# A streaming-encoder trunk: values read into their own tiles, an embedding in two halves, a shared norm tile, a free list of raw buffers, pair evictions at high priority

## The chip, the cores and the metric

The kernel runs on one core of one Trainium2 chip. The core has a matrix engine (TensorE, in the profile PE, with its weight loads as PEld), a vector engine (VectorE, DVE), a scalar or activation engine (ScalarE, ACT), GpSimd (POOL) and SyncE (SP), which here only issues transfers. Each engine runs its own instructions in the order in which they stand in its queue, and waits on semaphores for the others. Sixteen DMA engines move data between HBM and the on-chip memory. The metric is the device time of one execution in microseconds; the time before is the median of three.

## What is computed

Two layers (DEPTH 2) work on 512 frames of width 1024, in float32. Cut to what matters:

```python
for i in range(DEPTH):
    h = rmsnorm(x, norm1_g[i])
    z = h @ w_in[i] + b_in[i]        # mLSTM q k v o i f, retention q k v g, two branch gates
    y_m = sigmoid(mo) * headnorm(mlstm(mq, mk, mv, mi, mf))        # 4 heads of 256
    y_r = silu(rg) * headnorm(retention(rope(rq), rope(rk), rv))   # 4 heads, values of 512
    merged = sigmoid(gm) * (y_m @ w_bm[i]) + sigmoid(gr) * (y_r @ w_br[i])
    x = x + merged @ w_out[i]
    h2 = rmsnorm(x, norm2_g[i])
    x = x + square(relu(h2 @ w_ff1[i] + b_ff1[i])) @ w_ff2[i] + b_ff2[i]
    h3 = rmsnorm(x, norm3_g[i])
    x = x + sigmoid(h3 @ w_pe_gate[i]) * (p[i] @ w_pe[i])          # the embedding: p[i] has 256 columns
return rmsnorm(x, final_g)
```

## The kernel before

**Products.** Every float32 operand is split into a high and a low half of type fp32r, and a product is three matmuls: high by high, high by low, low by high (`mm3`, L440). The high half is written by ACT as a copy, the low half by DVE as a subtraction (`split`, L284: ACT L286, DVE L287).

**Units.** All weights stream from HBM once, in the order of `unit_list` (L160 and on). A T8 unit is 128 output columns by 1024 rows (`t8`, L451). A PAIR unit makes 256 output columns with seven products of half the size in place of eight (the Winograd form of Strassen's scheme, `run_pair`, L474). Its weights come in three raw tiles A, C and B; a fourth, D, is formed on chip. Its products P1, P5, P6, P2, P3, P7 and P4 are of 12 matmuls of 256 columns each and share three PSUM banks: a is used by P1, P6, P7 and P4 in turn, c by P5 and P3, b by P2. A product that starts anew in a bank that another has filled waits until that one is evicted. P4 is deferred: it is put on the list `later`, and `flush` runs it after P1 and P5 of the next pair, or inside the next T8. The retention values of two heads are a WIDE unit (`run_wide`, L513), the embedding has two PE units.

**Weights on their way.** `fill_raws` (L361) loads raw tiles through SP's queue; there are four buffers (RAWS, tag wr) and, until w_out, one more (wrx). `prep_next` (L389) runs LOOK = 2 units ahead: it splits a raw tile into the halves that PE reads, and for a pair adds parts of A and C into B (L421) and forms D (L424). The sums of weight blocks that the pairs need are made in HBM by accumulating transfers, which POOL issues at a pace set by PE (L331).

**Evictions.** For a projection pair `pair_tiles` (L541) empties the banks into two tmp tiles: P1, P5, P6 and P4 by ACT (L548, L550, L554, L560), P2, P3 and P7 by DVE (L552, L556, L558). For a pair of the second feed-forward matrix `add` in `ff2` (L1394) adds each bank into x on DVE (L1400). The ring of tmp tiles has six (NTMP). These instructions stand on ACT's and DVE's queues among the splits of the next weights. The order on each engine is that of a list scheduler, which follows the order of the program unless a priority is given.

**Retention.** The values of heads 1 and 3 are made with those of heads 0 and 2 and wait in HBM (rv_spill, written at L1166). `rv_load` (L1192) reads them back: for each of four row tiles it takes a tmp tile, issues a load on POOL's queue (L1197), and splits the tile into the value tiles that the head before has used. In the order of a layer (L1283 and on), head 0 is attended, its gates made, then `rv_load(1)`; head 2 is attended, r_qk(3) and the eight tiles br of the first half of w_br are made, each copied by ACT (L1301) and stored to br_spill by a transfer on ACT's queue (L1302), and then comes `rv_load(3)`, scores, and the gates and outputs of head 2 (`r_out`), whose pairs the trace calls l0r2o0 and l0r2o1. In the same way l0r0o0 is the first gate pair of head 0; l0r1brq and l0r1brk are head 1's query and key pairs.

**Norms.** A norm's sum of squares (tag ssum, written at L630 to L642) and its spread factor (tag rb, L702) are two tiles of 512 columns in a pool that lives throughout.

**End of a layer.** The feed-forward pairs of the last block come after the two embedding units (L1443): eight tiles of six matmuls with 512 columns, copied to `pe` by ACT. The four pairs l0o30 to l0o33 follow, then `flush` runs the last pair's P4, and after it the last two tiles of the third norm's operand are made (`tile3`, L1388). The gate projection w_pe_gate uses them at once; its evictions use the six or seven tmp tiles of a new pool.

## Time and profile before

| | |
|---|---|
| median of 3 runs | 2348.01 us (2347.84 to 2348.44) |
| the profiled execution | 2347.49 us |
| its span in the profile | 2345.8 us |
| granted TensorE clock, mean over the span | 0.997 |
| PE busy | 99% of the span, 13,660 matmuls |
| DVE, ACT, POOL busy | 73%, 52%, 10% |
| moved by DMA | 394.89 MB, 168 GB/s in the mean |

Times in the profile are counted from the span's start. A busy engine is one that has an instruction running; matmuls overlap, so two that follow each other start sooner than the first one's shown duration. In the table of waits a row says which instruction of PE stood idle, for which other engine's instruction, for how long in total, how often, and the longest. In a timeline row come start, duration, engine, line, operation, the tile written and the tiles read; in brackets, the idle time before it and what ended that. A row of windows gives the busy time of each engine in a stretch, the clock that TensorE was granted (1.00 is full), the busy share of the DMA engines and the rate in GB/s.

### The profile page before, as it was taken

How to read it: one execution, taken by the hardware profiler on the slowest of the kernel's cores; microseconds unless marked ns; L12 is line 12 of the kernel's file. 1: busy time of each engine (PE TensorE's matmuls, PEld its weight loads, DVE VectorE, ACT ScalarE, POOL GpSimd, SP SyncE). 2: the span in 40 equal slices, each digit the busy share in tenths (PEclk: the TensorE clock that was granted, in tenths of full speed). 3: DMA queues.
4: the chain of work that ended last, by engine and by line, in shares of the span. 5: the costliest groups of instructions: out<-in, count | busy, mean ns of one | idle time of the engine just before them, and what ended most of it. 6: DMA issues, size and time to landing. Idle time of an engine off the chain costs nothing. (4 is left out here: it accounts for less than half of the span.)

```text
span 2345.8 us, 35261 instructions
## 1 busy us (share of the span) xinstructions
PE 2320.2 (99%) x13660; PEld 2056.2 (88%) x13660; DVE 1722.9 (73%) x2658; ACT 1218.9 (52%) x1768; POOL 245.7 (10%) x369
## 2 busy tenths in 40 slices
PE   9999999999999999999999999999999999999998
PEld 7888899898898898899888888998989988998997
DVE  7878767895675577677878787778958656776785
ACT  6656444553554445446557564454536445445454
POOL 3111101100102100000321110000000020000012
PEclk9999999999999999999999999999999999999999
DMA  5666676667578667676775645434343542433431
GB/s 201 187 180 172 218 229 170 205 189 202 168 230 269 195 198 189 199 219 181 206 221 169 182 124 186 136 126 158 108 158 104 166 153 96 130 108 98 132 117 59
DMA packets 146631, 394.89 MB, mean 168 GB/s; under 512 B 15376, under 2 KB 18832, under 8 KB 146464
## 3 DMA queue, kind: packets, MB, share of 16 engines
q1 hardware_dynamic: 99952, 247.77, 32.0%
q0 software_dynamic: 31104, 117.45, 20.4%
q10 hardware_dynamic: 15408, 27.43, 3.3%
q8 instruction: 107, 1.75, 0.3%
q14 instruction: 60, 0.49, 0.1%
HBM read 373.71 MB, written 123.73 MB: 212 GB/s over the span
## 5 line engine op out<-in xcount | busy, mean ns | idle before, releaser
L286 ACT ACTIVATE wh<-wr 128x1024 fp32r<-128x1024 f32 (+1 forms) x223 | 232.2, 1044 | 276.5 <-issue 69.6
L287 DVE TENSOR_TENSOR wl<-wr,wh 128x1024 fp32r<-128x1024 f32 (+1 forms) x221 | 271.9, 1232 | 77.7 <-ACT wh L286 77.5
L286 ACT ACTIVATE wh_B<-wr 128x1024 fp32r<-128x1024 f32 x100 | 105.9, 1059 | 159.2 <-PE l0f L443 8.5
L287 DVE TENSOR_TENSOR wl_B<-wr,wh_B 128x1024 fp32r<-128x1024 f32 x100 | 121.9, 1219 | 32.5 <-ACT wh_B L286 32.3
L286 ACT ACTIVATE wh_D<-wr 128x512 fp32r<-128x512 f32 x76 | 48.0, 632 | 124.9 <-DVE wr L424 65.4
L286 ACT ACTIVATE wh_C<-wr 128x1024 fp32r<-128x1024 f32 x76 | 80.2, 1056 | 61.3 <-issue 9.2
L286 ACT ACTIVATE wh_A<-wr 128x1024 fp32r<-128x1024 f32 x76 | 79.9, 1052 | 54.7 <-PE l1f L443 9.0
L287 DVE TENSOR_TENSOR wl_C<-wr,wh_C 128x1024 fp32r<-128x1024 f32 x76 | 94.3, 1240 | 18.7 <-ACT wh_C L286 18.5
L287 DVE TENSOR_TENSOR wl_A<-wr,wh_A 128x1024 fp32r<-128x1024 f32 x76 | 92.7, 1220 | 17.3 <-ACT wh_A L286 17.3
L442 PE MATMUL l1f<-l1n2h,wh 128*128 128x512 f32 x256 | 99.8, 390 | 0.0
L442 PE MATMUL l0f<-l0n2h,wh 128*128 128x512 f32 x256 | 99.8, 390 | 0.0
L444 PE MATMUL l0f<-l0n2h,wl 128*128 128x512 f32 x256 | 99.7, 389 | 0.0
L444 PE MATMUL l1f<-l1n2h,wl 128*128 128x512 f32 x256 | 99.7, 389 | 0.0
L443 PE MATMUL l1f<-l1n2l,wh 128*128 128x512 f32 x256 | 99.6, 389 | 0.0
L443 PE MATMUL l0f<-l0n2l,wh 128*128 128x512 f32 x256 | 99.6, 389 | 0.0
L287 DVE TENSOR_TENSOR wl_D<-wr,wh_D 128x512 fp32r<-128x512 f32 x76 | 52.4, 689 | 33.2 <-ACT wh_D L286 31.7
L421 DVE TENSOR_TENSOR wr<-wr,wr 128x512 f32<-128x512 f32 x76 | 52.1, 686 | 14.6 <-DMA wr<-wpairs 13.1
L444 PEld LDWEIGHTS l0f<-l0n2h,wl 128*128 128x128 f32 x256 | 48.0, 188 | 10.2
L444 PEld LDWEIGHTS l1f<-l1n2h,wl 128*128 128x128 f32 x256 | 48.1, 188 | 10.1
L443 PEld LDWEIGHTS l1f<-l1n2l,wh 128*128 128x128 f32 x256 | 48.1, 188 | 9.8
L442 PEld LDWEIGHTS l0f<-l0n2h,wh 128*128 128x128 f32 x256 | 48.1, 188 | 9.8
L442 PEld LDWEIGHTS l1f<-l1n2h,wh 128*128 128x128 f32 x256 | 48.1, 188 | 9.7
(5625 smaller groups left out, 8357.9 us busy)
## 6 DMA issues: line engine op xcount, KB each, us to landing
wr<-wstream SPq DMA_DIRECT2D x219, 512.0 KB, 4.2
wr<-wpairs SPq DMA_DIRECT2D x228, 256.0 KB, 2.8
wr<-wwide SPq DMA_DIRECT2D x24, 512.0 KB, 4.0
s0t<-wwide POOLq DMA_DIRECT2D x5, 1024.0 KB, 7.8
s4t<-wwide POOLq DMA_DIRECT2D x5, 1024.0 KB, 9.0
s12t<-wwide POOLq DMA_DIRECT2D x5, 1024.0 KB, 8.1
s16t<-wwide POOLq DMA_DIRECT2D x5, 1024.0 KB, 8.5
s1t<-wpairs POOLq DMA_DIRECT2D x4, 1024.0 KB, 6.7
```

Of the source, the lines that this page charges most:

```text
L286: a = ac.activation(hi_ap, src, AF.Copy)
L287: return a, ve.tensor_sub(lo_ap, src, hi_ap.bitcast(F32))
L421: ve.tensor_tensor(raws[n, "B"][:, Q:], kept.pop((n, "A"))[:, Q:], r[:, :Q], OP.add)
L442: te.matmul(o, sh, mh, start=first, stop=False)
L443: te.matmul(o, sh, ml, start=False, stop=False)
L444: cur["mm"] = te.matmul(o, sl, mh, start=False, stop=last)
```

## The change

It has five parts. (1) `rv_load` becomes `rv_fetch`, which issues the four loads straight into the low tiles of the values, right behind the attend that has used them, and `rv_split`, which splits them in place after the next head's scores; no tmp tile is used. (2) The embedding is in two halves: `embed(0)` before the last four feed-forward pairs, `embed(1)` behind them, and the last pair's P4 runs after the second tile of `embed(1)`. The order of the weight units follows. (3) A norm's sum and spread share one tile of 1024 columns (`nr`), handed from norm to norm (`own`). While no norm needs it, from the unit rv0 to w_out, it is a raw buffer for weights ("one"). (4) Raw buffers are an explicit list: four of the weight pool, "low" and "one"; `give` returns a buffer when its last reader has been issued, and the next load takes the first that fits. (5) Pair evictions and the adds of `ff2` are issued at a priority of 250 ahead of their place in the program.

```diff
...
 LOOK = 2
+AHEAD = 250
 WARM = 11
...
     u.append(("PE", 0))
+    pairs(ff_order()[1])
     u.append(("PE", 1))
-    pairs(ff_order()[1])
     full("w_pe_gate")
...
     room = unit_list(0).index(("T8", "w_out", 0, 0))
-    cur["room"], cur["more"] = (), None
+    wide0 = unit_list(0).index(("WIDE", (0, "rv0"), 0))
+    where = {n + i * NU // L: ("low", "one") if n >= wide0 else ("low",) for i in range(L) for n in range(room)}
+    free, taken = ["low", "one"] + list(range(RAWS)), {}
+
+    def norm_tile():
+        return opool.tile([P, 2 * T], F32, name="nr", tag="nr", bufs=1)
+
+    def raw_tile(a):
+        if a == "one":
+            return norm_tile()
+        pl, tag = (cur["low"], "wrx") if a == "low" else (wpool, f"wr{a}")
+        return pl.tile([P, UN], F32, name=f"wr{at['load']}", tag=tag, bufs=1)
...
-    def fill_raws(most=RAWS + 1):
-        while at["load"] < len(loads) and len(raws) + len(kept) < most:
+    def fill_raws(most=None):
+        while at["load"] < len(loads) and at["load"] != most:
             n, x = loads[at["load"]]
-            r = None
-            if n in cur["room"] and cur["more"] not in raws:
-                cur["more"] = n, x
-                r = cur["low"].tile([P, UN], F32, name=f"wr{at['load']}", tag="wrx", bufs=1)
-            elif len(raws) - (cur["more"] in raws) >= RAWS:
+            fits = where.get(n, ()) if n * L // NU == cur["layer"] else ()
+            a = next((a for a in free if a in range(RAWS) or a in fits), None)
+            if a is None:
                 break
-            raws[n, x] = r = r or wpool.tile([P, UN], F32, name=f"wr{at['load']}", tag="wr", bufs=RAWS)
+            free.remove(a)
+            taken[n, x] = a
+            raws[n, x] = r = raw_tile(a)
             if x:
...
         fill_raws()
+
+        def give(*a):
+            free.extend(taken.pop(k) for k in a)
...
             kept[n, x] = r
+        elif x == "D":
+            give((n, "B"))
         elif x == "C":
...
             ve.tensor_tensor(raws[n, "B"][:, Q:], kept.pop((n, "A"))[:, Q:], r[:, :Q], OP.add)
+            give((n, "A"), (n, "C"))
         elif x == "B":
...
             formed[n, ("t4", x[1])] = t
+            give((n, ("t2", x[1])), (n, x))
+        elif not wide or x[0] != "t4":
+            give((n, x))
...
+    def ahead():
+
+        return tc.high_priority(AHEAD)
+
     def pair_tiles(name, act, consume, y=None):
...
         def done(x, o):
+            with ahead():
+                evict(x, o)
+            if x == "P4":
+                consume(y)
+
+        def evict(x, o):
             if x == "P1":
...
                 ac.activation(y[0][:, a], o, AF.Copy)
-                consume(y)
...
-        def __init__(self, name, i, gain, act=None, j0=0, j1=NT):
+        def __init__(self, name, i, gain, act=None, j0=0, j1=NT, own=None):
+            self.own = own
             self.name, self.i, self.gain = name, i, gain
...
             if self.sum is None:
-                pl = cur["last"] if self.half else opool
-                sq = pl.tile([P, w if self.half else T], F32, name=f"{self.name}sum", tag="ssum", bufs=1)[:, :w]
+                if self.half:
+                    sq = cur["last"].tile([P, w], F32, name=f"{self.name}sum", tag="ssum", bufs=1)
+                else:
+                    self.own = self.own or norm_tile()
+                    sq = self.own[:, 0:w]
             else:
...
             te.matmul(o[:, :w], ones_r, dl, start=False, stop=True)
-            pl = cur["last"] if self.half else opool
-            self.b = pl.tile([P, w if self.half else T], F32, name=f"{n}rb", tag="rb", bufs=1)[:, :w]
+            self.b = self.own[:, T:T + w]
             ac.activation(self.b, o[:, :w], AF.Copy)
...
     cur["tmp"], cur["ntmp"] = cur["low"], NTMP
-    cur["room"] = range(room)
+    cur["layer"] = 0
     n1 = Norm("l0n1", 0, "g1", acts(xa_pool, "l0n1"))
...
             cur["tmp"], cur["ntmp"] = cur["low"], NTMP
-            cur["room"] = range(i * NU // L, i * NU // L + room)
+            cur["layer"] = i
         cur["br"] = phase(f"br{i}", ph_side)
...
-        def rv_load(h):
+        def rv_fetch(h):
...
             for j in range(NT):
-                t = tmp(f"l{i}r{h}vr{j}")
-                gp.dma_start(t, rv_dram[i, h // 2, j])
-                split(t, v[0][j][:, :T], v[1][j][:, :T])
+                gp.dma_start(v[1][j][:, :T].bitcast(F32), rv_dram[i, h // 2, j])
             return v
+
+        def rv_split(v):
+            for hi, lo in zip(*v):
+                split(lo[:, :T].bitcast(F32), hi[:, :T], lo[:, :T])
...
         num = r_attend(0, pt, vv)
+        vv = rv_fetch(1)
         gs = {}
         r_gates(0, 0, gs)
-        vv = rv_load(1)
         pt = r_scores(1, qk)
+        rv_split(vv)
         yr = acts(cur["br"], f"l{i}yr0")
...
         num = r_attend(2, pt, vv)
+        vv = rv_fetch(3)
         qk = r_qk(3)
...
             nc.scalar.dma_start(br_dram[i, c], t[:, :T])
-        vv = rv_load(3)
         pt = r_scores(3, qk)
+        rv_split(vv)
         yr = acts(cur["br"], f"l{i}yr1")
...
                 y = x[2 * p + q // 2][:, (q % 2) * S:(q % 2 + 1) * S]
-                if b == 0 and q not in started:
-                    started.add(q)
-                    ve.scalar_tensor_tensor(y, y, bcol(i, "bf2", 2 * p + q // 2), o, OP.add, op)
-                else:
-                    ve.tensor_tensor(y, y, o, op)
+                with ahead():
+                    if b == 0 and q not in started:
+                        started.add(q)
+                        ve.scalar_tensor_tensor(y, y, bcol(i, "bf2", 2 * p + q // 2), o, OP.add, op)
+                    else:
+                        ve.tensor_tensor(y, y, o, op)
...
         n3_pool = phase(f"n3{i}", act_side)
-        n3 = Norm(f"l{i}n3", i, "g3", acts(n3_pool, f"l{i}n3"))
+        n3 = Norm(f"l{i}n3", i, "g3", acts(n3_pool, f"l{i}n3"), own=n2.own)
...
         pe = n3_pool.tile([P, KT, T], F32, name=f"l{i}pe", tag="pe")
-        for u in range(2):
+
+        def embed(u):
             _, wh, wl = unit("PE")
...
                 ac.activation(pe[:, 4 * u + c, :], o, AF.Copy)
+                if c == 1:
+                    flush()
+
+        embed(0)
         for _, b, p in rest:
             ff2(b, p)
-        flush()
+        embed(1)
         shift(cur["ff"], ph_side, False)
...
         cur["tmp"], cur["ntmp"] = phase(f"pg{i}", ph_side), 7
-        nn = ([Norm(f"l{i}n4{a}", i, "gf", None, 2 * a, 2 * a + 2) for a in range(2)] if last
-              else [Norm(f"l{i + 1}n1", i + 1, "g1", acts(xa_pool, f"l{i + 1}n1"))])
+        nn = ([Norm(f"l{i}n4{a}", i, "gf", None, 2 * a, 2 * a + 2, n3.own) for a in range(2)] if last
+              else [Norm(f"l{i + 1}n1", i + 1, "g1", acts(xa_pool, f"l{i + 1}n1"), own=n3.own)])
```

## The prediction

> **What bounds the kernel now.** I read the page's totals, then the table of waits for PE, then windows and timelines around the largest of them.

> ```profile
> span 2345.8 us, 35261 instructions
> PE 2320.2 (99%) x13660; PEld 2056.2 (88%) x13660; DVE 1722.9 (73%) x2658; ACT 1218.9 (52%) x1768; POOL 245.7 (10%) x369
> ```

> PE is busy for 2320.2 us of 2345.8. The change leaves its 13,660 matmuls as they are, so only PE's idle time, 2345.8 − 2320.2 = 25.6 us, and what a lowered clock adds to the busy time can go. What ends the idle time:

> ```profile
> engine line waited for: us in total, times, longest us
> PE l0r2o1a L491 <- ACT wh_A L286: 3.4, 1, 3.4
> PE l1o33a L491 <- DVE l1x L1400: 1.6, 1, 1.6
> PE l0o33a L491 <- DVE l0x L1400: 1.3, 1, 1.3
> PE l0m0vp L747 <- DVE wl L287: 1.3, 1, 1.3
> PE l0r0o0a L491 <- DVE l0r0o0y L558: 1.2, 1, 1.2
> PE l1r0o0a L491 <- DVE l1r0o0y L558: 1.2, 1, 1.2
> ...
> PE l0r1brqa L491 <- DVE l0r1brqy L558: 1.0, 1, 1.0
> ...
> PE l0o12a L491 <- DVE l0x L1400: 0.7, 1, 0.7
> ...
> PE l1r2o0a L491 <- ACT l1r2o0y L548: 0.5, 1, 0.5
> ...
> PE l1r2o1a L491 <- DVE l1r2o1y L558: 0.3, 1, 0.3
> PE l0r2o1a L491 <- DVE l0r2o1y L558: 0.2, 1, 0.2
> ```

> No row names a weight load on SP's queue. PE waits for splits and evictions, which queue behind one another on ACT and DVE. The largest, at 600 us:

> ```profile
> core 0: us, PE busy (x) PEld busy (x) DVE busy (x) ACT busy (x) POOL busy (x), PEclk, DMA share, GB/s
> 596.00:602.00 6.00, 4.38 (x37) 4.18 (x35) 3.45 (x6) 2.41 (x4) 1.10 (x2) 1.00 1.04 398
> 602.00:609.00 7.00, 4.86 (x21) 4.57 (x22) 5.36 (x11) 4.04 (x8) 0.00 (x0) 0.53 0.53 189
> 604.00:612.00 8.00, 7.64 (x45) 7.35 (x46) 5.58 (x11) 3.38 (x8) 0.00 (x0) 0.67 0.26 72
> 1129.00:1135.00 6.00, 5.63 (x30) 4.69 (x31) 4.24 (x6) 2.38 (x4) 1.30 (x1) 1.00 0.58 182
> ```
> ```profile
> 598.58 0.63 ACT L286 ACTIVATE l0r3vh<-l0r3vr 128x512 fp32r<-128x512 f32 x1 [2.83 <-DMA l0r3vr<-rv_spill]
> 602.16 0.63 ACT L286 ACTIVATE l0r3vh<-l0r3vr 128x512 fp32r<-128x512 f32 x1 [0.37 <-DMA l0r3vr<-rv_spill]
> 602.69 1.04 ACT L286 ACTIVATE wh_A<-wr 128x1024 fp32r<-128x1024 f32 x1
> 604.95 0.36 ACT L548 ACTIVATE l0r2o0y<-l0r2o0a 128x256 f32<-128x256 f32 x1
> ...
> 603.78 0.58 PE L491 MATMUL l0r2o1a<-l0xnh,wh_A 128*128 128x256 f32 x1 [3.40 <-ACT wh_A L286]
> 605.36 0.58 PE L491 MATMUL l0r2o0a<-l0xsh,wh_B 128*128 128x256 f32 x1 [0.35 <-ACT l0r2o0y L548]
> ...
> DMA to landing us min/median/max: 4.4/11.1/12.1
> ```

> ACT takes its instructions in order, and ahead of the split of wh_A stand four splits of values that `rv_load(3)` reads back (two are shown), while DMA is at 1.04; their loads land a median 11.1 us after issue (the last row, of tile l0r3vr). The weight split PE needs stands behind them. After the 3.4 us the clock is low: 0.67 over the eight us 604:612, a loss of (1 − 0.67) × 8 = 2.6 us. With the 0.35 that follows the site costs 3.4 + 0.35 + 2.6 = 6.4. After the 1.3 us wait near 1129 the clock is 1.00, so shorter waits cost only themselves.

> [...]

> **The change part by part.**

> *Values into their own tiles.* The four loads of a head's values move from after the gates (layer's r1) or after the br loop (r3) to right behind the attend whose value tiles they overwrite, and need no tmp slot. All are issued by POOL, and each now waits there until PE has read the tile, so sums transfers and norm operations queued behind wait too; POOL is busy 10% of the span and no row of waits names a late sum, so I cost this at nothing (uncovered, it holds one sums transfer for the rest of an attend, 2.3 us below). What the loads meet there, and what a split costs:

> ```profile
> core 0: us, PE busy (x) PEld busy (x) DVE busy (x) ACT busy (x) POOL busy (x), PEclk, DMA share, GB/s
> 404.00:408.00 4.00, 4.00 (x36) 4.00 (x35) 4.00 (x10) 2.27 (x5) 1.21 (x3) 1.00 0.34 98
> 528.00:532.00 4.00, 4.00 (x33) 3.88 (x33) 2.45 (x7) 2.06 (x4) 1.27 (x2) 1.00 0.30 85
> ...
> DMA to landing us min/median/max: 2.9/3.4/3.7
> 595.92 0.28 PE L491 MATMUL l0r2o0a<-l0xnh,wh_A 128*128 128x256 f32 x1
> 597.36 0.28 PE L491 MATMUL l0r2o0c<-l0xsh,wh_A 128*128 128x256 f32 x1
> 591.62 0.39 PE L443 MATMUL l0br<-l0yr0l,wh 128*128 128x512 f32 x1
> 591.85 0.39 PE L444 MATMUL l0br<-l0yr0h,wl 128*128 128x512 f32 x1
> ```

> At r3 the loads go from the 1.04 share to 0.30 (window 528:532), some 65 us before the splits. The splits then wait for nothing, the weight raw ahead of them no longer shares its DMA, and 600 us loses its 6.4. I leave 0.5 there: an eviction's tmp slot still hangs on a br store of that crowded stretch (bounds 0 to the 3.4 of today). At r1 the loads are late next to their splits. One product is 12 matmuls, 597.36 − 595.92 = 1.44 us. In the new order ACT has the first value split, then P1's eviction of l0r0o0 (0.36), then three value splits, then P5's eviction. P1's bank is wanted two products, 2.9 us, after attend's last matmul; that attend tile has 12 matmuls of 512 columns, 0.23 us apart (591.85 − 591.62), and the first value tile is read by its second, so the load goes 10 × 0.23 = 2.3 us before the end. So PE has 2.3 + 2.9 − 0.63 − 0.36 = 4.2 us for a landing which took 3.4 (median row above, tile l0r1vr): it fits. But three splits, 3 × 0.63 = 1.9 us, now stand ahead of P5's eviction and of the next weights. I give three places per layer (the deferred brk P4, the P3 behind weight C, the own P4) half of today's 1.2 us wait each: 3 × 0.6 = 1.8, in two layers 3.6 (bounds 0 and 3 × 1.2 × 2 = 7.2; the half, since each has a product of cover).

> *Evictions ahead of splits.* High priority moves pair evictions and ff2's adds in front of weight splits on ACT and DVE. The case to see, last ff2 pair of layer 0:

> ```profile
> 1126.67 0.41 DVE L1400 TENSOR_TENSOR l0x<-l0x,l0o33c 128x256 f32<-128x256 f32 x1
> 1127.01 1.98 DVE L287 TENSOR_TENSOR wl<-wr,wh 128x1024 fp32r<-128x1024 f32 x1
> 1128.91 0.41 DVE L1400 TENSOR_TENSOR l0x<-l0x,l0o33a 128x256 f32<-128x256 f32 x1
> 1129.37 0.38 PE L491 MATMUL l0o33a<-l0hh,wh_D 128*128 128x256 f32 x1 [1.35 <-DVE l0x L1400]
> ```

> A weight split of 1.98 us stands ahead of the 0.41 us add that frees P4's bank. Ahead of it, the add is done 1.98 us earlier. What becomes late is the split itself, by 0.41; its weights are wanted two units on, so that is covered (uncovered: 0.41 for each overtaking). This takes the P4 waits of r0o0 (2 × 1.2), o12 (0.7), r2o0 and r2o1 (0.5 + 0.3 + 0.2) and brq (1.0, where the add that forms the weights also comes sooner): 2.4 + 0.7 + 1.0 + 1.0 = 5.1, at the r0 sites against the 3.6 above.

> *Embedding in halves.* Four of its eight output tiles now follow the last pair, and the pair's deferred P4 runs after two of them. Each tile is 6 matmuls of 512 columns, so two are 12 × 0.23 = 2.7 us, more than the 1.6 and 1.3 us that PE waits at o33: both go, 2.9 us. The first ff2 pair has only half of the embedding ahead of it, 24 × 0.23 = 5.5 us instead of 11, as cover for its weight split and the norm's operands: 0.3 a layer, 0.6 given back (bounds 0 and 1.3, the wait at o33 turned round).

> *Norm's tile and the free list.* A sixth raw buffer from the values' first unit to w_out, loads as tiles come free. PE names no load today, so I cost it at nothing by itself: its cover is the two-unit lookahead. It helps at 600 us, counted there. Gone wrong, the shared tile's wait for the norm's last reader would hold SP's whole queue of weights: bounds −1 (the brq row) and +1.3 (the m0vp row, a wait of PE for a split). The m0vp wait and the tail stay.

> *Sum.* Removed 6.4 + 5.1 + 2.9 = 14.4; given back 0.5 + 3.6 + 0.6 = 4.7; net −9.7. The profiled execution took 2347.49 (span 2345.8, 1.7 outside it), giving 2337.8. The median of the runs, 2348.01, stands 0.5 higher: forecast 2338.

> **The rivals.**

> *The in-order queue (slower).* Splits now wait in place for loads into their own tile, with evictions behind them on ACT. At r1 the room is 4.2 us. Were the landing the 11.1 us measured at 600 us, a site would stall 11.1 − 4.2 = 6.9 us and halve the clock once more, 9.5 in all. Against a net −9.7 one such site leaves no change, two (l0r1, l1r1) give 2338 + 19 = 2357. It decides from a landing of 4.2 us on; the sign flips at two sites with about 4.2 + (9.7 − 5.2) / 2 = 6.5 us. For it: ACT waited 2.83 us for such a load at 598 us. Against it: the share of 0.34 at 404:408 and the 3.4 us landing there. [...]

> *The 600 us site stays.* br stores of the same stretch hold tmp slots, and the weight raw still comes late there. Then the 6.4 is not won: 2338 + 5.9 = 2344. For it: the 1.04 share is not only the value loads. Against: the weight split ran straight after the value splits, without a wait of its own.

> *The change doesn't do what it says.* Evictions come sooner but the splits they pass become what PE waits for: the 5.1 and 2.9 come back at the next pair, and r1's and the halves' costs stay. 2338 + 8 = 2346, no change.

> **How the numbers follow.** Forecast 0.70 (its own range 2332 to 2344: r1's bounds −3.6 and +3.6, the 0.5 and 0.6 won or the latter at 1.3, raw buffer −1 and +1.3), 600 us site 0.12, no effect 0.08, in-order queue 0.10. A measurement of this kernel can tell about 0.2%, 4.7 us, from no change: faster is below 2343.3, slower above 2352.7. Faster: the forecast and a third of the 600 us site, 0.74; same: the rest of it, no effect, and a single late site, 0.17; slower 0.09. The range reaches from 2331 (all lower bounds, 2338 − 3.6 − 0.5 − 0.6 − 1 = 2332.3, and 1 for runs that differ) to 2348, past the two rivals that end short of no change, and leaves out the two-site stall.

> **What would show it.** Right: no PE row for wh_A at 600 us and a clock of 1.00 there; no o33 rows; small rows at r0o0 of both layers, with value splits ahead of P5's eviction on ACT; landing of the values under 4.2 us at r1. Wrong: ACT rows waiting for rv_spill with an eviction behind them; a new window with a clock under 0.8; PE waits of over 1.2 us for split weights right behind overtaking evictions; SP's loads waiting on the norm's tile. The forecast fails if PE's idle time doesn't fall from 25.6 to about 25.6 − (9.7 − 2.6) = 18.5 us.

## The result and the profile after

The changed kernel takes 2356.0 us (median of 6 runs, 2354.61 to 2358.45) against 2348.0 beside it (2347.78 to 2349.22): a ratio of 1.0033, with the 95% interval 1.0021 to 1.0045. It is slower by 8 us where 2338 was forecast. The page of the profiled execution begins:

```profile
span 2354.3 us, 35247 instructions
PE 2322.2 (99%) x13660; PEld 2058.3 (87%) x13660; DVE 1725.1 (73%) x2658; ACT 1218.1 (52%) x1768; POOL 243.8 (10%) x369
```

PE's idle time rose from 25.6 to 2354.3 − 2322.2 = 32.1 us. The table of waits for PE, after (total, times, longest, in us):

```profile
PE l0r3o1a L512 <- DVE l0r3o1y L589: 4.1, 1, 4.1
PE l0o11a L512 <- DVE l0x L1438: 2.5, 1, 2.5
PE l1r3o1a L512 <- DVE l1r3o1y L589: 1.8, 1, 1.8
PE l0o21a L512 <- DVE l0x L1438: 1.7, 1, 1.7
...
PE l0o22a L512 <- DVE l0x L1438: 1.2, 1, 1.2
...
PE l0o12a L512 <- DVE l0x L1438: 1.0, 1, 1.0
PE l1r0o0c L512 <- ACT l1r0o0y L581: 0.8, 1, 0.8
PE l0o21a L514 <- DVE wl_A L288: 0.8, 1, 0.8
...
PE l0r0o0c L512 <- ACT l0r0o0y L581: 0.6, 1, 0.6
```

The old rows are gone: no wh_A at 600 us, no o33, no brq. In their place stand P4 of l0r3o1 and l1r3o1, and in the feed-forward pairs P7 and P4 behind adds into x, and first products behind a weight split, wl_A. The windows around the old and the new largest wait, with the clock as the third number from the end:

```profile
604.00:612.00 8.00, 8.00 (x70) 8.00 (x69) 5.12 (x8) 5.30 (x10) 0.00 (x0) 1.00 0.33 99
642.00:648.00 6.00, 2.41 (x22) 2.17 (x20) 1.81 (x3) 1.06 (x1) 0.00 (x0) 1.00 0.76 253
648.00:656.00 8.00, 7.45 (x50) 7.45 (x51) 7.07 (x12) 4.88 (x10) 0.00 (x0) 0.79 0.00 1
```

At 604:612 the clock is back at 1.00 from 0.67. It is low after the new wait instead: (1 − 0.79) × 8 = 1.7 us on top of the 4.1.

To see what each place won or lost, waits and clock together, I use one measure from here on. The **loss** of a site is the sum, over its matmuls, of the distance from the start of the matmul ahead, less the median distance for matmuls as wide as that one in the same run. Over all matmuls it is 42.7 us before and 51.4 after; the difference of 8.6 is that of the spans (8.5).

| loss, us | before | after | predicted change |
|---|---|---|---|
| l0r2 (the 600 us site) | 7.9 | 1.3 | −6.1 with r2's small rows |
| l1r2 | 2.4 | 1.3 | −0.8 |
| l0r1 | 2.3 | 0.7 | −1.0 |
| l0r0 and l1r0 | 6.0 | 6.0 | +1.2 |
| o33, both layers | 3.4 | 0.6 | −2.9 |
| o30, both layers | 0.0 | 0.6 | +0.6 |
| other ff2 pairs, layer 0 | 2.1 | 9.4 | −0.7 |
| other ff2 pairs, layer 1 | 0.1 | 2.5 | 0 |
| l0r3 | 0.6 | 6.5 | 0 |
| l1r3 | 0.6 | 4.0 | 0 |

The first six rows come out within 1.2 us of the forecast. (Of the +1.2 one part was for brk's deferred P4, whose matmuls count as r1; nothing came there.) The last four add 7.3 + 2.4 + 5.9 + 3.4 = 19 us, where the forecast had a gain of 0.7.

The values' loads themselves came in time, as the sum had it. ACT at r1, and the landing of the loads of tile l0r1vl:

```profile
404.36 0.63 ACT L287 ACTIVATE l0r1vh<-l0r1vl 128x512 fp32r<-128x512 f32 x1
...
407.00 0.63 ACT L287 ACTIVATE l0r1vh<-l0r1vl 128x512 fp32r<-128x512 f32 x1 [0.43 <-DMA l0r1vl<-rv_spill]
407.54 0.37 ACT L581 ACTIVATE l0r0o0y<-l0r0o0c 128x256 f32<-128x256 f32 x1
...
DMA to landing us min/median/max: 2.8/3.1/3.5
```

P5's eviction at 407.54 stands behind the splits, and that is the price there: the 0.6 and 0.8 of the two r0o0c rows, 0.9 and 1.1 as losses. The P4 waits that went (l0r0o0a and l1r0o0a, from 1.5 each to 0.5 and 0.3 as losses) are worth about as much, so the row of r0 doesn't move.

**Where DVE waits now.** In the table of waits for DVE the row of the add that forms weight B (L421 before, L438 after) grew from 13.1 us in 11 waits to 23.3 in 18. DVE waited for weight loads before, too. At one place PE felt it: the add at 384.81 waited 3.72 us with P3's and P7's evictions of l0r1brq behind it, and that is the 1.0 of the brq row of PE. The rows before, then the row after:

```profile
DVE wr L421 <- DMA wr<-wpairs: 13.1, 11, 3.7
...
384.81 0.69 DVE L421 TENSOR_TENSOR wr<-wr,wr 128x512 f32<-128x512 f32 x1 [3.72 <-DMA wr<-wpairs]
...
386.88 0.41 DVE L558 TENSOR_TENSOR l0r1brqy<-l0r1brqa,l0r1brqy 128x256 f32<-128x256 f32 x1
...
DVE wr L438 <- DMA wr<-wpairs: 23.3, 18, 4.6
```

Two new places show what it holds up. DVE at l0r3o1, after:

```profile
642.86 0.42 DVE L587 TENSOR_TENSOR l0r3o1y<-l0r3o1c,l0r3o1y 128x256 f32<-128x256 f32 x1
647.47 0.69 DVE L438 TENSOR_TENSOR wr<-wr,wr 128x512 f32<-128x512 f32 x1 [4.19 <-DMA wr<-wpairs]
648.08 0.42 DVE L589 TENSOR_TENSOR l0r3o1y<-l0r3o1a,l0r3o1y 128x256 f32<-128x256 f32 x1
```

P7's last matmul ended at 643.5, and its eviction (L589) needs 0.42. It stands behind a forming add for which DVE waits 4.19 us. By the order of the splits this add belongs to the second pair of gr, l0gr1, which PE starts only at 673.4; that of the first pair ran at 626.29 without a wait. In the ff2 pairs, DVE and then PE after, at l0o11:

```profile
933.16 0.42 DVE L1438 TENSOR_TENSOR l0x<-l0x,l0o10a 128x256 f32<-128x256 f32 x1
938.14 0.69 DVE L438 TENSOR_TENSOR wr<-wr,wr 128x512 f32<-128x512 f32 x1 [4.57 <-DMA wr<-wpairs]
938.75 0.68 DVE L288 TENSOR_TENSOR wl_D<-wr,wh_D 128x512 fp32r<-128x512 f32 x1
939.36 0.41 DVE L1438 TENSOR_TENSOR l0x<-l0x,l0o11a 128x256 f32<-128x256 f32 x1
...
929.08 0.39 PE L514 MATMUL l0o11a<-l0hh,wl_A 128*128 128x256 f32 x1 [0.77 <-DVE wl_A L288]
939.82 0.39 PE L512 MATMUL l0o11a<-l0hh,wh_C 128*128 128x256 f32 x1 [2.46 <-DVE l0x L1438]
```

and the same stretch of DVE before:

```profile
934.81 0.42 DVE L1400 TENSOR_TENSOR l0x<-l0x,l0o11a 128x256 f32<-128x256 f32 x1
...
936.28 0.41 DVE L1400 TENSOR_TENSOR l0x<-l0x,l0o11b 128x256 f32<-128x256 f32 x1
936.61 0.68 DVE L421 TENSOR_TENSOR wr<-wr,wr 128x512 f32<-128x512 f32 x1
```

Before, P6's add stood ahead of the forming add; now it stands behind. An eviction at high priority ended up behind an instruction without any, which then waited for a load that was issued at 929 and landed at 938. The order fits a scheduler that counts on the load being there sooner; that reason is argued, not shown. Nor does the order follow the program where no priority is given: in the kernel before, the forming add of l0gr0 already stands five instructions ahead of the split of its A on DVE, which the program issues before it.

### The profile page after: what moved, and what is told of

It reads as the page before. It is cut to its first block, busy times and chain, and to the rows that moved or that the text cites. A ratio compares the mean times of both kernels' runs of the same rounds, so it can differ in the third digit from the quotient of the medians.

```text
span 2354.3 us, 35247 instructions
## 1 busy us (share of the span) xinstructions
PE 2322.2 (99%) x13660; PEld 2058.3 (87%) x13660; DVE 1725.1 (73%) x2658; ACT 1218.1 (52%) x1768; POOL 243.8 (10%) x369
## 4 chain that ended last, share of the span: by engine, by line
PE 82%; issue 8%; DVE 5%; DMA 2%; ACT 1%; POOL 0%; DVEq 0%; ACTq 0%; POOLq 0%
PE l0f L463 2%; PE l1f L463 2%; PE l1f L464 2%; PE l0f L464 2%; PE l1f L465 2%; PE l0f L465 2%; DMA wr<-wpairs 2%; PE l1br L463 1%; PE l0br L463 1%; PE l1br L465 1%; PE l0br L465 1%; PE l0br L464 1%; PE l1br L464 1%; PE l0pg L463 1%; PE l0bm L463 1%
## 5 line engine op out<-in xcount | busy, mean ns | idle before, releaser
L287 ACT ACTIVATE wh<-wr 128x1024 fp32r<-128x1024 f32 (+1 forms) x213 | 221.4, 1043 | 277.2 <-issue 69.6
L288 DVE TENSOR_TENSOR wl<-wr,wh 128x1024 fp32r<-128x1024 f32 (+1 forms) x211 | 260.0, 1234 | 77.7 <-ACT wh L287 76.8
L287 ACT ACTIVATE wh_B<-wr 128x1024 fp32r<-128x1024 f32 x86 | 90.9, 1057 | 108.0 <-PE l0bm L464 8.8
L288 DVE TENSOR_TENSOR wl_B<-wr,wh_B 128x1024 fp32r<-128x1024 f32 x86 | 105.0, 1220 | 17.5 <-ACT wh_B L287 17.0
L287 ACT ACTIVATE wh_D<-wr 128x512 fp32r<-128x512 f32 x66 | 41.6, 630 | 124.7 <-DVE wr L442 61.5
L287 ACT ACTIVATE wh_C<-wr 128x1024 fp32r<-128x1024 f32 x66 | 69.7, 1057 | 67.6 <-PE l0br L464 8.0
L287 ACT ACTIVATE wh_A<-wr 128x1024 fp32r<-128x1024 f32 x76 | 79.9, 1052 | 47.9 <-PE l1f L464 6.7
L288 DVE TENSOR_TENSOR wl_C<-wr,wh_C 128x1024 fp32r<-128x1024 f32 x66 | 82.2, 1245 | 19.6 <-ACT wh_C L287 19.1
L288 DVE TENSOR_TENSOR wl_D<-wr,wh_D 128x512 fp32r<-128x512 f32 x66 | 45.5, 690 | 32.5 <-ACT wh_D L287 31.6
L438 DVE TENSOR_TENSOR wr<-wr,wr 128x512 f32<-128x512 f32 x56 | 38.6, 690 | 26.0 <-DMA wr<-wpairs 23.3
L465 PEld LDWEIGHTS l0f<-l0n2h,wl 128*128 128x128 f32 x256 | 48.1, 188 | 10.2
L464 PEld LDWEIGHTS l0f<-l0n2l,wh 128*128 128x128 f32 x256 | 48.1, 188 | 9.8
```

The source lines that it names most:

```text
L287: a = ac.activation(hi_ap, src, AF.Copy)
L288: return a, ve.tensor_sub(lo_ap, src, hi_ap.bitcast(F32))
L438: ve.tensor_tensor(raws[n, "B"][:, Q:], kept.pop((n, "A"))[:, Q:], r[:, :Q], OP.add)
L464: te.matmul(o, sh, ml, start=False, stop=False)
L465: cur["mm"] = te.matmul(o, sl, mh, start=False, stop=last)
```

## The experiments

Twelve kernels, each timed against the kernel before on the same chip. All share the changed kernel's code except for the edit shown. Losses are of one profiled execution each. Medians of different experiments can come from different chips, on which the kernel before took 2348.0 to 2349.0 us; the ratios are free of that. Line numbers shift by a few with the edits.

**Without the high priority**, everywhere, or in ff2 only:

```diff
-            with ahead():
-                evict(x, o)
+            evict(x, o)
...
-                with ahead():
+                if True:
                     if b == 0 and q not in started:
```

> The changed kernel with pair evictions and ff2 adds at their usual priority; all else stays. Theory (hoisted add): the high priority, with the sixth raw buffer, lets DVE's add that forms weight B (L438) stand earlier in its queue, where it waits for a weight load and holds the evictions behind it. Then the rows l0r3o1a (4.1), l1r3o1a (1.8) and the o11, o12, o21, o22, o32 rows (about 10 together with the wl_A rows) go, and the time falls from 2356 to 2338 to 2342. Rival (late loads): the free list itself makes raw tiles land later; then DVE's waits at L438 stay near 23 us and the time stays at 2353 to 2357.

> The changed kernel with high priority for the projections' pair evictions only, not for ff2's adds. Theory: all rows of o11, o12, o21, o22, o32 and wl_A at o11 and o21 go (10.7 us), o12 comes back with 0.7; l0r3o1a stays: 2346. Rival (late loads): 2354 to 2357, with DVE's waits for loads at the ff2 pairs as now.

Measured: 2346.1 us (ratio 0.9994, 0.9985 to 1.0002) without any priority, 2344.8 (0.9984, 0.9975 to 0.9993) without it in ff2. In both, the other ff2 pairs' loss falls from 9.4 and 2.5 to about 1.1 in each layer: the priority on ff2's adds is that loss. Theory and time of the second hold. The first came out 4 us above its expectation, and for a reason that tells: l0r3 and l1r3 stay at 6.0 and 2.8. The priority isn't what holds P7's eviction there. Between the two kernels only the priority on the projections' pairs differs; in the profiled executions it is worth 10.2 − 6.0 at r0 and 1.9 − 0.4 at gr, 5.7 us, so there the fifth part does what it says; the medians, 1.3 us apart with overlapping intervals, put less on it.

**Without the sixth buffer**, the norm's tile never a raw buffer:

```diff
-    where = {n + i * NU // L: ("low", "one") if n >= wide0 else ("low",) for i in range(L) for n in range(room)}
+    where = {n + i * NU // L: ("low",) for i in range(L) for n in range(room)}
```

> The changed kernel without the norm's tile as a raw buffer (free list of five). Theory (hoisted add): L438 of the unit at l0r3o1 stands 8 instead of 24 places ahead of the split of its A, so l0r3o1a and l1r3o1a lose their 4.1 and 1.8 us and the clock loss with them, 7 in all: 2349; the ff2 rows stay. Rival (the high priority alone does it): 2356, the rows stay. Rival (late loads from fewer buffers): slower than 2356.

Measured: 2349.9 (1.0008, 0.9999 to 1.0017). l0r3 and l1r3 fall to 0.8 each, l0r1 goes back from 0.7 to 2.3, the ff2 losses stay (11.2 and 1.4). So the r3 loss belongs to the sixth buffer: with it the forming add of l0gr1 stands one place ahead of P7's eviction and 18 places ahead of the split of its own A in DVE's order, with or without priority; without it, 15 places behind that eviction and 3 ahead of the split.

**The forming add pinned** behind the split of the C that it reads, in all pairs:

```diff
-            ve.tensor_tensor(raws[n, "B"][:, Q:], kept.pop((n, "A"))[:, Q:], r[:, :Q], OP.add)
+            f = ve.tensor_tensor(raws[n, "B"][:, Q:], kept.pop((n, "A"))[:, Q:], r[:, :Q], OP.add)
+            tc.add_manual_dep(f.ins, cur["prep"][1].ins.name, ORDER, reason="order of the weights")
```

> The changed kernel with one more order: L438 stands on DVE behind the split of the C tile that it reads. Theory (hoisted add): the evictions no longer wait behind it: l0r3o1a and l1r3o1a go (7 us) and the P6 waits of the ff2 pairs (7); the four wl_A rows of 0.8 stay: about 2341. Rival (late loads): C's split waits in its place and the time stays at 2353 to 2357.

Measured: 2360.8 (1.0053, 1.0040 to 1.0065), slower than the change itself and above both forecasts. At r3 the theory holds (1.1 and 1.1). In ff2 it falls: layer 0 loses 11.9, o33 in both layers 5.5, and new rows appear, for B's split, which now comes late itself; the wait at l0o21 stays:

```profile
PE l0o21a L513 <- DVE l0x L1439: 2.0, 1, 2.0
...
PE l1o33a L515 <- DVE wl_B L288: 0.8, 1, 0.8
```

The position of that one add isn't the whole of the ff2 loss.

**Both parts out** (priority on ff2 and sixth buffer), and, in the other way, the buffer kept and the forming add ordered behind its A for gr's first pair alone:

```diff
+            if units[n][1:] in (((0, "gr"), 0), ((1, "gr"), 0)):
+                tc.add_manual_dep(f.ins, cur["A"].ins.name, ORDER, reason="order of the weights")
```

> The changed kernel with neither the high priority on ff2's adds nor the norm's tile as a raw buffer. Theory (two separate losses: ff2's adds overtaking splits, and the sixth buffer drawing the add that forms B ahead of P7's eviction at r3): both go; of the run without priority on ff2 the l0r3 and l1r3 losses (5.4 and 2.8 us above an unhindered PE) fall to 0.8 each, l0r1 and the r2 sites come back with 2.4: 4 to 5 us below that run, 2339 to 2341. Rival (one loss seen twice): no further gain, 2344 to 2346.

> The changed kernel without the priority on ff2's adds, the sixth buffer kept, and one order added in each layer: for the first pair of gr alone, the add that forms B (L438) stands behind the split of its A on DVE. Theory (this one add holds P7's eviction at r3o1): l0r3 and l1r3 fall from 5.4 and 2.8 to about 0.8 each, everything else stays as without the priority: 2337 to 2339. Rival (the loads are late themselves): the wait moves to the pair of gr and the time stays at 2344 to 2346.

Measured: 2338.5 (0.9954, 0.9942 to 0.9967) and 2340.0 (0.9958, 0.9946 to 0.9971). Without both parts the two losses go together with them, as two separate ones; l0r3 is 0.7, l1r3 1.5 (0.7 of it for an eviction at brq), and the time is what was forecast for the whole change. With the one order added, l0r3 and l1r3 fall from 5.4 and 2.8 to 0.8 each. The add that was pinned, l0gr0's, isn't the one that held P7's eviction, but with it the scheduler put l0gr1's add behind that eviction, where it waits 2.51 us for its load as before (2.71 without the pin):

```profile
642.50 0.42 DVE L592 TENSOR_TENSOR l0r3o1y<-l0r3o1a,l0r3o1y 128x256 f32<-128x256 f32 x1 [0.25 <-PE l0r3o1a L517]
645.43 0.69 DVE L439 TENSOR_TENSOR wr<-wr,wr 128x512 f32<-128x512 f32 x1 [2.51 <-DMA wr<-wpairs]
```

So the two runs differ at this site in which of the two stands first, and the loss goes with that. But in layer 0 part of it moved, as its rival said:

```profile
PE l0gr1a L517 <- DVE wl_B L288: 1.7, 1, 1.7
PE l0gr0a L515 <- ACT l0gr0y L582: 1.4, 1, 1.4
```

gr loses 3.9 there in place of 0.2. At gr0 it is still the wait of l0gr1's add: behind it on DVE stand r3's outputs, ACT waits 2.77 us for them at 646.82, and P1's eviction (L582) stands behind that on ACT. At gr1 the split of B stands behind the forming add of the pair after, which waits 3.13 us for a load at 669.46. In layer 1 nothing came back.

**The old reading of values**, and **the embedding whole**, each on the kernel without priority on ff2 (at both sites of a layer, and with the units' order to match):

```diff
-        vv = rv_fetch(3)
...
+        vv = rv_load(3)
         pt = r_scores(3, qk)
-        rv_split(vv)
```

```diff
         embed(0)
+        embed(1)
         for _, b, p in rest:
             ff2(b, p)
-        embed(1)
+        flush()
```

> The changed kernel without the priority on ff2's adds, and with rv_load of before in place of rv_fetch and rv_split. Theory (the early fetch took the 600 us wait away): l0r2's loss goes from 1.3 back to about 7.9 us, and r1's rows with it: 6 to 7 above the run with the fetch, 2350 to 2352. Rival (the raw buffers or the evictions took it away): l0r2 stays under 2.5 and the time at 2343 to 2347.

> The changed kernel without the priority on ff2's adds, and with the embedding whole ahead of the last four pairs. Theory (the second half covers the last P4): the o33 waits of 1.3 and 1.6 us come back, o30's 0.3 each go: 2 to 3 above the run with halves, 2347. Rival (another part took o33 away): no change, 2344 to 2345.

Measured: 2347.9 (0.9996, 0.9987 to 1.0005) and 2345.8 (0.9985, 0.9976 to 0.9994). With rv_load, l0r2's loss is 6.5 in place of 1.3, and the wait at 600 us is back on the same split:

```profile
PE l0r2o1a L512 <- ACT wh_A L287: 2.9, 1, 2.9
```

The early fetch, not the sixth buffer, took it away, though the buffer was there in this run. The expected 2350 was too high by 2: r1's rows didn't come back, and l0r0 and l1r0 lose 5.0 in place of 6.0, so the early fetch costs about 1.0 there. With the embedding whole, o33 loses 3.4 again in place of 0.3, and o30 nothing in place of 0.8: by the losses the halves are worth 3.1 − 0.8 = 2.3 us. By their medians, 1.0 apart with overlapping intervals, the two kernels can't be told apart.

**Priority for some of ff2's adds**: those of P1, P5, P6 and P7, on the kernel without the sixth buffer.

```diff
-                with ahead():
+                with ahead() if first else ExitStack():
...
-                    add(1, o, OP.add)
+                    add(1, o, OP.add, x_ == "P1")
```

> The changed kernel without the norm's tile as a raw buffer, with high priority in ff2 only for the adds of P1, P5, P6 and P7, after which PE reuses the bank within the pair; the adds of P2, P3 and P4 keep their place. To be held against the run without the sixth buffer (2349.9, ff2 losses of 3.7 at l0o11, 3.8 at l0o21, 0.7 and 1.0 in layer 1). Theory A (on a full DVE the adds of P2 and P3 overtake the weight splits, about 0.35 us each): the wl_A rows fall from 0.8 to about 0.4 and the l0o11 and l0o21 losses below 2: 2344 to 2347. Theory B (the add that forms B is drawn ahead by any priority in ff2 and then waits for its load): the rows of l0o11 and l0o21 on DVE's l0x stay near 2.4 and the time at 2348 to 2350.

Measured: 2347.8 (0.9994, 0.9985 to 1.0003). The wl_A rows are halved in three of four places, as theory A has it. Of the rows behind the add into x that of l0o11 falls from 2.4 to 1.3, that of l0o21 doesn't fall (2.3 without this edit):

```profile
PE l0o21a L512 <- DVE l0x L1438: 2.5, 1, 2.5
```

Neither theory alone.

**The sixth buffer only up to w_br**, without priority on ff2:

```diff
-    where = {n + i * NU // L: ("low", "one") if n >= wide0 else ("low",) for i in range(L) for n in range(room)}
+    wbr = unit_list(0).index(("T8", "w_br", 0, 0))
+    where = {n + i * NU // L: ("low", "one") if wide0 <= n < wbr else ("low",) for i in range(L) for n in range(room)}
```

> The changed kernel without the priority on ff2's adds, and with the norm's tile as a raw buffer only up to the first unit of w_br, so before r3's outputs. Theory: the sixth buffer's gain at l0r1 (2.6 against 0.7 without it) stays and its loss at l0r3 and l1r3 doesn't come: 1.5 to 2.5 below the run without the buffer, 2336 to 2337.5. Rival (its gain and loss hang together, since the free list's order carries on): l0r3 over 2 and 2339 to 2344.

Measured: 2336.9 (0.9947, 0.9935 to 0.9960), faster than the kernel before by 12 us and than the changed kernel by 19. l0r1 keeps 0.7, l0r3 and l1r3 are 0.7 and 0.8, as its theory had it. The two longest waits of PE are of 1.3 us each. Its gain over the kernel without both parts (2338.5) is within the intervals.

**On that best kernel, ff2's priority put back**, and with it the forming add of ff2's pairs pinned behind the split of its A:

```diff
-                if True:
+                with ahead():
...
+            if units[n][1][1][:2] == "ff":
+                tc.add_manual_dep(f.ins, cur["A"].ins.name, ORDER, reason="order of the weights")
```

> The best kernel so far (2336.9: no priority on ff2's adds, sixth raw buffer only up to w_br) with the one line put back: priority on all of ff2's adds. It measures that part alone. Theory (the priority on ff2 costs 10 us whatever the rest does): ff2's losses rise by 7 in layer 0 and 2.5 in layer 1, 2345 to 2348. Rival (the loss needs the sixth buffer at r3 or another part): 2337 to 2340.

> The same with priority on ff2's adds and, for ff2's pairs alone, the add that forms B (L438) ordered behind the split of its A, so that P6's add stands ahead of it. Theory hoisted add: only the wl_A rows stay (4 times 0.8), the DVE l0x rows of l0o11, l0o21 and l0o22 go: 2339 to 2341. Theory late loads (splits overtaken on a full DVE end later, raw tiles come free later and SP, in order, loads the next pair later): the wait moves from L438 to C's split and the evictions behind it, l0o11 and l0o21 keep more than 2 each: 2343 to 2348; layer 1, where no sums are loaded beside it, loses only the 0.8s.

Measured: 2346.8 (0.9991, 0.9981 to 1.0001) and 2351.3 (1.0010, 1.0001 to 1.0019). The one line costs 10 us by the medians; the losses, of one execution each, rise by 8.4 in layer 0 (1.0 to 9.3) and not in layer 1 (1.2 and 1.0: there the 0.8s at wl_A replace other small ones), where 2.5 was expected. Pinning makes it worse again, above both forecasts: layer 0 at 10.3, layer 1 at 3.6, o33 at 3.3. The pair of kernels without and with the line shows how the loss begins. DVE and SP around l0o11, whose first matmul is at 922.6 without it:

```profile
919.87 0.69 DVE L288 TENSOR_TENSOR wl_D<-wr,wh_D 128x512 fp32r<-128x512 f32 x1
...
930.43 0.69 DVE L439 TENSOR_TENSOR wr<-wr,wr 128x512 f32<-128x512 f32 x1
...
920.58 0.33 SPq L392 DMA_DIRECT2D wr<-wpairs  x1
```

and at 920.8 with it:

```profile
920.33 0.68 DVE L288 TENSOR_TENSOR wl_D<-wr,wh_D 128x512 fp32r<-128x512 f32 x1
...
930.04 0.69 DVE L439 TENSOR_TENSOR wr<-wr,wr 128x512 f32<-128x512 f32 x1 [3.48 <-DMA wr<-wpairs]
...
921.04 0.33 SPq L392 DMA_DIRECT2D wr<-wpairs  x1
```

Counted from that matmul, D's split starts 2.7 us ahead without the line and 0.5 ahead with it, because adds and an operand split of ff1 now stand before it. Its end frees the raw buffer into which SP loads the next pair's first tile: 2.0 us ahead, or 0.2 behind. The next tiles follow on the same queue. The load for which the forming add waits, the first half of tile C, is issued at +0.4 without the line (922.99) and at +1.4 with it (922.18). Between the two, at +0.6 in both kernels, POOL issues one of the accumulating transfers that make the sums, at its pace set by PE. Without the line, that transfer, then the load and the time it takes to land:

```profile
923.23 0.89 POOL L332 DMA_DIRECT2D s15t<-wpairs  x1 [13.68 <-PE l0o10a L515]
...
L392 SPq DMA_DIRECT2D wr<-wpairs x1: 328/328/328, 923.0 to 923.0; - x1
...
DMA to landing us min/median/max: 2.7/2.7/2.7
```

and with it, with who waited for the load:

```profile
921.41 0.89 POOL L332 DMA_DIRECT2D s15t<-wpairs  x1 [13.39 <-PE l0o10a L515]
...
L392 SPq DMA_DIRECT2D wr<-wpairs x1: 328/328/328, 922.2 to 922.2; - x1
...
  DVE wr L439: 3.5, 1
...
DMA to landing us min/median/max: 7.8/7.8/7.8
```

Just ahead of the transfer the load takes 2.7 us, just behind it 7.8. The forming add runs at +7.8 without a wait, or waits until +9.2 after DVE has come to it at about +5.8. So the priority does three things at once: it brings DVE to the add 2 us sooner, it makes the load 1 us later, and by that puts it behind the transfer, which costs 5 us more. The last is the largest. An estimate from these rows: had the load landed in 2.7 us again, it would have been there at 924.9, before DVE came to the add at 926.6.

The fourteen kernels agree at l0o11 and at l0o21. In the eight without priority on ff2's adds this load is issued 0.1 to 0.2 us ahead of POOL's transfer and lands in 2.5 to 2.9 us; in the six with it on all or some of them, 0.4 to 3.5 us behind, and lands in 6.5 to 9.0 us (9.0 at l0o11 of the changed kernel). In layer 1 no such transfer runs at these pairs (the changed kernel issues the last of them at 1367.5 us, and its l1o11 begins at 2094.2), and the same add waits for nothing there (2100.03 and 2184.24, no idle time before either). That the transfer is what slows the load is read from these rows; no run moved the transfer alone. Pinned, the add gives its raw tiles back later, the load of C is issued at +4.0 and still takes 7.6 us, and other splits become late.

## Why the prediction was wrong, point by point

**What bounds the kernel, and the 600 us site: right.** PE waited for splits and evictions queued on ACT and DVE. l0r2's loss fell by 6.6, clock included, where 6.1 was forecast, and the run with rv_load brought the wait back. One of the small r2 rows was misread: the 0.5 of l1r2o0a is P6 behind P1's eviction on ACT (L548), not a P4; it went with the others.

**r1: right in kind, too dear.** Evictions behind value splits were given 3.6 us against 2.4 removed; l0r0 and l1r0 stayed at 6.0 together. The three places per layer were one, P3 on P5's eviction, at 0.6 to 0.8 of wait and 0.9 to 1.1 of loss. And the 1.0 that l0r1brq was to win by the evictions' priority came by the sixth buffer: l0r1 loses 2.3 to 2.6 without it and 0.7 to 1.0 with it (1.9 with the adds pinned), and 1.0 is the figure without any priority.

**Embedding in halves: right.** −2.8 and +0.6 against −2.9 and +0.6.

**Evictions ahead of splits: right in the projections by the losses, wrong in ff2, and this is one failed step.** The prediction put the overtaken split's lateness at 0.41 and called it covered by the two units of lookahead. On DVE in ff2, where operand splits of ff1 stand too, several adds overtake the same split, and it is no longer covered: PE waits 0.8 for wl_A at l0o11, l0o21 and in layer 1. And the split's end is not only what PE waits for. It frees the raw buffer, so the lateness goes on through SP's queue to the next pair's load. In layer 0 that load then falls behind a transfer of the sums and lands in 9.0 us where 2.8 was measured before, and the add that forms B waits for it on DVE, with the evictions behind it. The step "where a stall goes" ended at the split; it should have gone on to who waits for the buffer. The two layers differ as that says: layer 0, where sums are being made in HBM beside the loads, lost 7.3, layer 1 only 2.4, most of it the two waits for wl_A and one of 0.6 at l1o32.

**The sixth buffer at nothing: wrong, the other failed step.** "PE names no load today" was true and not enough. With the extra buffer l0gr1's third tile, B, into which the forming add writes, is loaded at 642.97 (without it at 653.48), and that add stands one place ahead of P7's eviction at l0r3o1 in place of 15 behind. There it waited 4.19 us for a load. That cost 5.9 and 3.4 us, for 1.6 to 1.9 gained at l0r1. The bound given, +1.3, came from a wait for a split and not from a wait for a load that blocks a queue, although the in-order rival stood two paragraphs below.

**The rival that won by its form.** An instruction that waits for a load with an eviction behind it in the queue of its engine was forecast to end slower, near 2357, at a chance of 0.10. It happened, on DVE with the forming add and weight loads (4.19 us of wait at l0r3o1, 4.57 at l0o11), not on ACT with value splits; the value loads landed in 3.1 us. That its 2357 lies beside the measured 2356 is chance: it came from two stalls of 9.5 us at l0r1 and l1r1, where nothing was lost. The order of instructions on DVE, before and after, showed the forming add moved up. I had read its move at l0r1 as a gain, and didn't ask what it waits for elsewhere, though the brq row of the kernel before was already this stall, on DVE.

With the two failed steps taken out, the rest of the change comes to 2338.5, the forecast of 2338 for the whole. That agreement is luck in part, since this kernel also lacks the priority in ff2 and the gain at l0r1: o12's loss falls from 0.9 to 0.5 without that priority, and l0r1 keeps 2.6 where 1.3 was forecast.

## What to carry to other kernels

When something is moved up a queue, follow the overtaken instruction past its direct reader: what buffer does its end free, which load waits for that, what else is in flight when that load is issued, and what stands behind its reader. An instruction that reads a fresh load must stand behind every eviction that PE needs: at l0r3o1 DVE kept its order, the eviction behind the add waited with it, and DVE's 4.19 us for a load became 4.1 us of PE. A priority didn't guarantee that order here. An extra buffer isn't free of risk either: give it to the stretch in which a wait shows its lack, and look at what it pulls forward elsewhere.

## What was not expected of the hardware

The prediction had read from one wait of 1.3 us that shorter waits cost only themselves. But the clock fell after shorter waits than the 3.4 us of before, and not after every one of the same length. In the run of the changed kernel PE waited 1.85 us at l1r3o1 and lost the clock, and waited 2.46 us at l0o11 and kept it. The windows are cut where the clock changed:

```profile
1815.06 0.39 PE L512 MATMUL l1r3o1a<-l1xnh,wh_D 128*128 128x256 f32 x1 [1.85 <-DVE l1r3o1y L589]
...
1812.57:1815.98 3.41, 1.56 (x13) 1.32 (x12) 2.00 (x4) 1.68 (x3) 0.00 (x0) 1.00 0.41 133
1815.98:1819.39 3.41, 3.41 (x18) 3.41 (x17) 3.41 (x6) 2.09 (x4) 0.00 (x0) 0.50 0.00 0
935.34:938.75 3.41, 2.02 (x18) 1.81 (x16) 0.60 (x1) 0.00 (x0) 0.00 (x0) 1.00 0.98 256
938.75:942.16 3.41, 2.34 (x19) 2.34 (x20) 3.39 (x6) 1.79 (x2) 0.19 (x1) 1.00 0.53 186
```
